# A two-layer decoder kernel on one core: the second chunk of the down weights in two parts, and the routing weights computed earlier

## The chip, the core and the metric

The kernel runs on one core of one Trainium2 chip. The core has a matrix engine (PE, with weight loads listed apart as PEld), three engines for elementwise work (DVE, ACT and POOL), and queues for DMA, most of which are issued by SP. Each engine works through its own instructions in the order in which they were written; semaphores make an instruction wait for another engine. The metric is the device time of one execution in microseconds (us).

## The reference

Two layers work on 512 tokens of width 1024, all in float32. Each layer has a mixing part (four mixers, one output projection), a mixture of experts, and a gated embedding. The change lies in the mixture of experts:

```python
def hier_moe(x, wg, bg, we, be, w_gate, w_up, w_down):
    gl = jnp.einsum("bsd,dg->bsg", x, wg, ...) + bg          # 4 groups
    pg = jax.nn.softmax(gl, axis=-1)
    c = jnp.argmax(gl, axis=-1)
    el = ...                                                 # 4 experts of the group
    pe = jax.nn.softmax(el_c, axis=-1)
    tv, ti = lax.top_k(pe, TOP_K_IN_GROUP)                   # 2 of them
    tv = tv / jnp.sum(tv, axis=-1, keepdims=True)
    wts = gc * tv
    ...
    for e in range(N_EXPERTS):                               # 16
        hdn = jax.nn.silu(x @ w_gate[e]) * (x @ w_up[e])     # 1024 -> 256
        y = y + combine[..., e:e + 1] * (hdn @ w_down[e])    # 256 -> 1024
```

## The kernel before

Tokens lie in four tiles of 128. After the routing (`route`, L1064) the kernel goes through the 16 experts in a fixed order (`experts`, L1282). For each it gathers up to 128 rows of its tokens from DRAM (an indirect DMA issued by POOL), transposes them on PE, multiplies by the gate and up weights, applies silu, multiplies by the down weights and scatters the result (another indirect DMA of POOL). Tokens beyond 128 of an expert go through `overflow`.

A matrix product is made in one of two ways. In the one (`mm3`, L254) both factors are split into a high part of type F32R and a low part, the difference, also F32R; three multiplies, high by high, high by low and low by high, are added up in PSUM. The high part of a weight tile is a cast on ACT (`whi_of`, L224), the low part a subtraction on DVE (`wlo_of`, L235). In the other way the product is one multiply of F32 tiles, which needs no splitting.

The weights come in units of 128x2048 F32 (1 MB), loaded by SP into rings of buffers (`wr` in the rows). An expert has three units: two of gate and up, each used as two halves of 128x1024, and one of down, whose first half (rows 0 to 127 of the 256) is split, and whose second half is used as F32. `_Weights.get` (L137) hands out the halves in order and makes high parts three halves ahead, low parts right after, into rings `wh` and `wl` of four tiles each.

The loop over e is skewed: iteration e does gate and up of expert e in four quarters q (six multiplies each), and the down product of expert e-1 at its end. After quarter 1, `down_in` (L1215) transposes the silu result `hs` of expert e-1; its first 128 columns are split into `hh` (a cast on ACT, a subtraction on DVE), its second 128 copied to `hT` (DVE). After quarter 3 come silu of expert e (`eth` on ACT, `ehs` twice on DVE) and the transposes and split of the next gathered rows (`xTh` on ACT, `xTl` on DVE, L222). Then `down` (L1229): for the first chunk of 128 rows, three F32R multiplies for each of the two halves of 512 columns (L255 to L257); for the second chunk, one F32 multiply for each half (L1241). ACT evicts the result (`ys`), POOL scatters it. Iteration 16 has the last expert's down product alone.

`weights` (L1131) computes the two weights of a token's experts, nine small operations on DVE and two exponentials on ACT; it is called at the start of iteration 2, and its result is first used in `combine` (L1330), after all experts.

The order of the work is the order of the program's text; no scheduler moves it.

Of the kernel before, what the change touches and what calls it, by code (L numbers as in the profile page):

```python
# [11 lines left out]
F32 = mybir.dt.float32  # L12
F32R = mybir.dt.float32r
# [154 lines left out]
class _Kernel:  # L168
# [895 lines left out]
    def route(self):  # L1064
        nc, V, G, T, SC, sm, l = self.nc, self.V, self.G, self.T, self.SC, self.sm, self.l
        iota, L, small = self.iota, self.L, self.small
        ep = self.ep = self.pool("ep", side=self.side[1])
        self.xg = [self.gpool.tile([128, D], F32, name=f"xg{j}", tag=f"gv{1 - j}") for j in range(2)]
        for j in range(2):
            G.memset(self.xg[j], 0.0)  # L1070
        self.yd = self.dram.tile([2 * S, D], F32, name=f"yd{l}")

        Cz = small([128, NT + 1, 16], "Cz", BF)
        G.memset(Cz[:, 0], 0.0)

        L5 = L.rearrange("p i (g e) -> p i g e", e=4)
        O1, O2 = small([128, NT, 5, 4], "O1"), small([128, NT, 4, 4], "O2")
        el = small([128, NT, 4, 4], "el")
        m1 = self.first_max(O1, L5, 5, "o1")
        V.scalar_tensor_tensor(el, O1[:, :, 1:], -BIG, L5[:, :, 1:], op0=ALU.mult, op1=ALU.add)  # L1080
        m2 = self.first_max(O2, el, 4, "o2")
        og = O1[:, :, 0, :, None].to_broadcast([128, NT, 4, 4])
        V.tensor_add(el, O1[:, :, 1:], O2)
        V.tensor_mul(Cz[:, 1:].rearrange("p i (g e) -> p i g e", e=4), el, og)
        OH = small([128, 2, NT, 16], "OH")
        for k, src in enumerate((O1[:, :, 1:], O2)):
            V.tensor_mul(OH[:, k].rearrange("p i (g e) -> p i g e", e=4), src, og)

        pc = self.mm([128, NT + 1, 16])
        T.matmul(pc, self.onesb, Cz, start=True, stop=False)  # L1090
        for j in range(2, NT + 1):
            T.matmul(pc[:, j:], self.onesb, Cz[:, 1:NT + 2 - j], start=False, stop=False)
        T.matmul(pc[:, 0:NT], self.trib, Cz[:, 1:], start=False, stop=True)

        OH8 = OH.rearrange("p k i e -> p (k i) e")
        RO = small([128, 8, 2, 16], "RO", F16)
        V.tensor_mul(RO, OH8[:, :, None, :].to_broadcast([128, 8, 2, 16]),
                     self.vtab[:, :, :, None].to_broadcast([128, 8, 2, 16]))
        pk = small([128, 8, 16], "pk")
        V.tensor_mul(pk.rearrange("p (k i) e -> p k i e", k=2), OH,  # L1100
                     pc[:, None, 0:NT].to_broadcast([128, 2, NT, 16]))
        pos = small([128, 8], "pos")
        V.tensor_reduce(pos, pk, axis=AX, op=ALU.add)
        SO = ep.tile([128, 8, 128], F16, name="SO", tag="ys", bufs=2)
        pidx = self.mm([128, 32])
        for a in (0, 4):
            V.tensor_tensor(SO[:, a:a + 4], iota[:, None, :].to_broadcast([128, 4, 128]),
                            pos[:, a:a + 4, None].to_broadcast([128, 4, 128]), op=ALU.is_equal)
            for j in range(a, a + 4):
                T.matmul(pidx, SO[:, j], RO[:, j].rearrange("p a e -> p (a e)"), start=(j == 0), stop=(j == 7))  # L1110
        ix = self.ix = self.mp.tile([128, 32], I32, name="ix")
        V.tensor_scalar(ix, pidx, NOIDX, None, op0=ALU.add)
        for e in range(2):
            self.gather(self.xg[e], ix[:, e:e + 1])

        nov = self.nov = small([128, NE], "nov")
        V.tensor_scalar(nov, pc[:, NT], 128.5, None, op0=ALU.is_ge)
        for lim in (256.5, 384.5):
            V.scalar_tensor_tensor(nov, pc[:, NT], lim, nov, op0=ALU.is_ge, op1=ALU.add)
        novs = small([128, 1], "novs")  # L1120
        V.tensor_reduce(novs, nov, axis=AX, op=ALU.add)
        self.novi = small([128, 1], "novi", I32)
        V.tensor_copy(self.novi, novs)
        self.cnt = small([128, 1], "cnt")
        V.memset(self.cnt, 0.0)
        self.w.make_lo()
        self.warm(WARM)
        self.OH8, self.pos = OH8, pos
        self.wt_in = L[:, :, 0:4], m1, m2, O1[:, :, 0]

    def weights(self):  # L1131

# [79 lines left out]
        self.V.tensor_mul(hs, hs, gu[:, 256:512])  # L1212
        return hs

    def down_in(self, hs, split=True):  # L1215

        pt = self.tr([128, 2, 128])
        for c in range(2):
            self.T.transpose(pt[:, c], hs[:, c * 128:(c + 1) * 128], self.ident)
        hT = self.ep.tile([128, 2, 128], F32, name="hT", bufs=2)  # L1220
        if not split:
            self.V.tensor_copy(hT, pt)
            return hT, None
        hh = self.ep.tile([128, 2, 128], F32R, name="hh", bufs=2)
        self.split(pt[:, 0], hh[:, 0], hh[:, 1])
        self.V.tensor_copy(hT[:, 1], pt[:, 1])
        return hT, hh

    def down(self, hT, w_, first=None):  # L1229

        hT, hh = hT
        ys = self.ep.tile([128, D], F32, name="ys", bufs=2)
        o = [self.mm([128, 512]) for _ in range(2)]
        for c in range(2):
            wc = first if first and not c else w_(c)
            for nh in range(2):
                ns = slice(nh * 512, (nh + 1) * 512)
                if first and not c:
                    self.mm3(o[nh], hh[:, 0], hh[:, 1], wc[0][:, ns], wc[1][:, ns], True, False)
                else:  # L1240
                    self.T.matmul(o[nh], hT[:, c], wc[:, ns], start=(c == 0), stop=(c == 1))  # L1241
        for nh in range(2):
            self.SC.activation(ys[:, nh * 512:(nh + 1) * 512], o[nh], AF.Copy, scale=0.5)  # L1243
        return ys

    def overflow(self):
# [4 lines left out]
        with tc.If(n_ov > 0) as _:  # L1251
            with tc.For_i(0, n_ov, 1) as _:
                ixo, eovi = self.block()
                ex = nc.values_load(eovi[:1, 0:1], engines=[mybir.EngineType.SP], min_val=0, max_val=NE - 1,
                                    skip_runtime_bounds_check_because="an expert's index")
                og = ep.tile([128, D], F32, name="og", tag="ys", bufs=2)
                G.memset(og, 0.0)
                self.gather(og, ixo[:, 0:1])
                oT = ep.tile([128, 8, 128], F32, name="oT", tag="xTh", bufs=1)
                for b in range(2):  # L1260
                    pt = self.tr([128, 4, 128])
                    for c in range(4):
                        T.transpose(pt[:, c], og[:, (4 * b + c) * 128:(4 * b + c + 1) * 128], self.ident)
                    V.tensor_copy(oT[:, 4 * b:4 * b + 4], pt)
                gu = self.mm([128, 512])

                def part(src, c):
                    w_ = ep.tile([128, 1024], F32, name="ow", tag="xTl", bufs=1)
                    src = src.rearrange("a p n -> p (a n)")
                    nc.sync.dma_start(w_, src[:, c * 1024:(c + 1) * 1024])  # L1270
                    return w_

                for q in range(4):
                    w_ = part(A["wgu"][l, bass.ds(ex, 1), q // 2], q % 2)
                    for c in range(2):
                        T.matmul(gu, oT[:, 2 * q + c], w_[:, c * 512:(c + 1) * 512], start=(q + c == 0), stop=(q + c == 4))
                hs = self.silu(gu)
                ys = self.down(self.down_in(hs, False), lambda c: part(A["wdn"][l, bass.ds(ex, 1)], c))
                self.scatter(ys, ixo[:, 1:2])


    def experts(self):  # L1282
# [12 lines left out]
        w.load(w.items[w.cur][0] + 1 + w.ahead, self.G)  # L1295
        prep(0)
        for e in range(NE + 1):
            if e == 2:
                self.weights()
            if e == NE - 1:  # L1300
                self.gbias = self.gvec(3 * l + 2, 1)
                self.pT = self.gpool.tile([128, 2, S], F32, name="pT", tag="gv0")
# [1 line left out]
            if e == NE - 1 and l + 1 < self.depth:  # L1304
                self.load_params(l + 1)
            if e < NE:
                hiT, loT = xT.pop(e)
                gu = self.mm([128, 512])
                for q in range(4):
# [3 lines left out]
                        self.mm3(gu, hiT[:, k], loT[:, k], hi[:, c], lo[:, c], k == 0, k == 7)  # L1313
                    if q == 1 and e > 0:
                        hT = self.down_in(hs)
                hs = self.silu(gu)
            else:
                hT = self.down_in(hs)
            if e + 1 < NE:
                prep(e + 1)  # L1320
            if e > 0:
                first, wd = w.get(), w.get()
                ys = self.down(hT, lambda c: wd[:, c * 1024:(c + 1) * 1024], first)
                si = self.scatter(ys, self.ix[:, 16 + e - 1:16 + e])
                for s_ in scat:
                    tc.declare_no_dep(si.ins, s_.ins, reason="rows of other tokens or ranks")
# [254 lines left out]
```

## Time and profile before

| | us |
|---|---|
| median of 3 runs (lowest, highest) | 904.88 (903.62, 905.17) |
| the profiled execution, its own time | 907.17 |
| its span from first to last instruction | 905.3 |
| PE busy in the span | 850.8 (94%) |
| DVE busy | 706.5 (78%) |
| ACT busy | 514.3 (57%) |
| POOL busy | 158.2 (17%) |

The experts of the two layers lie at about 229 to 388 and 671 to 830 us of the span. "Busy" is the time in which an engine executes; register work, semaphores and DMA issues don't count. A row of the timeline has the start, the time it took, engine, line, operation, the tile it writes and those it reads, the shape, the count, and in brackets the idle time before it and what ended that. Neighbouring rows overlap by a little, since an engine starts an instruction before the last one has drained; for PE the starts tell more than the durations. A row "x2" stands for two instructions one behind the other. An F32 multiply of 512 columns has two records, an F32R multiply one.

### The profile page before, as it was taken

What the parts mean: (1) busy time and instruction counts of PE and PEld (TensorE: products, weight loads), DVE (VectorE), ACT (ScalarE), POOL (GpSimd) and SP (SyncE); (2) the same over time, 40 slices, a digit from 0 to 9 for tenths busy, and PEclk for the clock granted to TensorE, in tenths of its full rate; (3) what the DMA queues carried; (4) which work ended last, traced back from release to release, by engine and by line L of the source; (5) the groups of instructions that cost most, each with busy time, mean ns of one, the idle gap of its engine ahead of it and who ended that gap; (6) DMA issues with size and microseconds to landing.
All of it is one profiled execution on the core that took longest, in us unless ns stands there. A gap on an engine that the chain in (4) does not pass through costs nothing. (4 is left out here: it accounts for less than half of the span.)

```text
span 905.3 us, 12251 instructions
## 1 busy us (share of the span) xinstructions
PE 850.8 (94%) x4393; PEld 683.9 (76%) x4393; DVE 706.5 (78%) x1182; ACT 514.3 (57%) x929; POOL 158.2 (17%) x214
## 2 busy tenths in 40 slices
PE   6999999997899999999979999999969999999994
PEld 5888877785677777777879887778847777777783
DVE  4499989966788888766676999898478888885674
ACT  4322348753677877755433232696447778777453
POOL 2050002122221221011010500112132122111201
PEclk8999999997999999999999999999979999999998
DMA  9322330157799979663322212210968998882702
GB/s 341 120 102 76 122 117 1 47 219 293 267 337 358 375 275 333 268 245 161 117 93 93 94 62 106 100 48 31 392 225 310 364 374 320 316 325 92 274 24 93
DMA packets 35776, 179.02 MB, mean 198 GB/s; under 512 B 8064, under 2 KB 8320, under 8 KB 18944
## 3 DMA queue, kind: packets, MB, share of 16 engines
q1 hardware_dynamic: 23472, 148.49, 43.7%
q0 software_dynamic: 9792, 20.99, 6.3%
q10 hardware_dynamic: 2448, 8.73, 2.6%
q8 instruction: 35, 0.57, 0.2%
q14 instruction: 29, 0.24, 0.1%
HBM read 171.89 MB, written 23.07 MB: 215 GB/s over the span
## 5 line engine op out<-in xcount | busy, mean ns | idle before, releaser
L239 DVE TENSOR_TENSOR wl<-wr,wh 128x1024 fp32r<-128x1024 f32 x212 | 253.2, 1221 | 43.0 <-ACT wh L228 41.8
L228 ACT CAST wh<-wr 128x1024 fp32r<-128x1024 f32 x212 | 216.4, 1053 | 89.9 <-PE mm L256 52.2
L255 PE MATMUL mm<-wh,xTh 128*128 128x512 f32 x256 | 114.4, 447 | 0.7 <-ACT xTh L221 0.7
L257 PE MATMUL mm<-wh,xTl 128*128 128x512 f32 x256 | 101.5, 396 | 1.2 <-DVE xTl L222 1.2
L256 PE MATMUL mm<-wl,xTh 128*128 128x512 f32 x256 | 100.9, 394 | 0.0
L483 DVE SCALAR_TENSOR_TENSOR acc<-glu,cwh,acc 128x512 f32<-128x512 f32 x120 | 91.7, 830 | 0.1
L257 PE MATMUL mm<-nhi,wl 128*128 128x512 f32 (+1 forms) x224 | 77.3, 345 | 2.6 <-DVE wl L239 2.6
L255 PE MATMUL mm<-nhi,wh 128*128 128x512 f32 (+1 forms) x224 | 77.1, 344 | 0.0
L256 PE MATMUL mm<-nlo,wh 128*128 128x512 f32 (+1 forms) x224 | 77.0, 344 | 0.0
L1198 POOL DMA_INDIRECT xg<-xnd,ix x32 | 35.3, 1105 | 150.2 <-PE tr L251 137.9
L255 PEld LDWEIGHTS mm<-wh,xTh 128*128 128x128 f32 x256 | 48.5, 190 | 16.7 <-issue 6.7
L1241 PE MATMUL mm<-wr,hT 128*128 128x512 f32 x128 | 60.2, 592 | 0.0
L256 PEld LDWEIGHTS mm<-wl,xTh 128*128 128x128 f32 x256 | 48.5, 190 | 15.4 <-DVE wl L239 6.2
L257 PEld LDWEIGHTS mm<-wh,xTl 128*128 128x128 f32 x256 | 48.3, 189 | 12.8 <-DVE xTl L222 2.7
L255 PE MATMUL mm<-wh,mhi 128*128 128x512 f32 x128 | 54.9, 429 | 0.0
L1203 POOL DMA_INDIRECT yd<-ys,ix x32 | 32.3, 1010 | 122.9 <-ACT ys L1243 107.3
L255 PE MATMUL mm<-wh,n3h 128*128 128x512 f32 x128 | 51.1, 399 | 0.0
L257 PE MATMUL mm<-wh,mlo 128*128 128x512 f32 x128 | 50.9, 397 | 0.0
L256 PE MATMUL mm<-wl,mhi 128*128 128x512 f32 x128 | 50.5, 394 | 0.0
L257 PE MATMUL mm<-wh,n3l 128*128 128x512 f32 x128 | 50.4, 394 | 0.0
L256 PE MATMUL mm<-wl,n3h 128*128 128x512 f32 x128 | 49.9, 390 | 0.0
L257 PEld LDWEIGHTS mm<-nhi,wl 128*128 128x128 f32 x224 | 42.4, 189 | 8.2 <-DVE wl L239 3.2
(235 smaller groups left out, 1851.2 us busy)
## 6 DMA issues: line engine op xcount, KB each, us to landing
wr<-wgu SPq DMA_DIRECT2D x62, 1024.0 KB, 9.1
wr<-wdn SPq DMA_DIRECT2D x30, 1024.0 KB, 13.4
wr<-win SPq DMA_DIRECT2D x13, 1024.0 KB, 9.4
wr<-wout SPq DMA_DIRECT2D x8, 1024.0 KB, 4.9
wr<-wpg SPq DMA_DIRECT2D x8, 1024.0 KB, 15.8
yt<-yd SPq DMA_DIRECT2D x12, 512.0 KB, 8.0
wr<-wqk SPq DMA_DIRECT2D x4, 1024.0 KB, 4.7
xnd<-xn ACTq DMA_DIRECT2D x8, 512.0 KB, 3.7
```

Source lines behind the costliest of these rows:

```text
L228: self.SC.copy(hi, src)
L239: self.V.tensor_sub(lo, src, h32)
L255: self.T.matmul(o, lh, rh, start=first, stop=False)
L256: self.T.matmul(o, lh, rl, start=False, stop=False)
L257: self.T.matmul(o, ll, rh, start=False, stop=last)
L483: V.scalar_tensor_tensor(acc[:, m], glu[:, m, k:k + S], self.cwh[:, m, k:k + 1], acc[:, m], op0=ALU.mult, op1=ALU.add)
L1198: return self.G.indirect_dma_start(out=dst, out_offset=None, in_=self.xnd[:, :], in_offset=bass.IndirectOffsetOnAxis(ap=col, axis=0), boun ...
L1203: return self.G.indirect_dma_start(out=self.yd[:, :], out_offset=bass.IndirectOffsetOnAxis(ap=col, axis=0), in_=src, in_offset=None, bound ...
L1241: self.T.matmul(o[nh], hT[:, c], wc[:, ns], start=(c == 0), stop=(c == 1))
```

## The change

For iterations 1 to 15 the second chunk of the down weights is also split in two parts and multiplied with `mm3`. A new function `down2` makes the parts, in two halves of 512 columns: both high parts are casts on ACT; the low part of the first half is a subtraction on POOL (`self.G`), that of the second half a subtraction on DVE. They have tiles of their own with one buffer each (`w2h0`, `w2l0`, `w2h1`, `w2l1`, in the rows of the order `w2h` and `w2l` with a number). The call for the first half stands after quarter 1 (behind `down_in`), that for the second after quarter 2. `down_in` splits both chunks of the transposed activations in these iterations, in one cast and one subtraction of 128x256, and makes no copy. Iteration 16, the last expert, and the overflow keep the old way. `weights()` is called at the end of `route` instead of at iteration 2.

```diff
         self.wt_in = L[:, :, 0:4], m1, m2, O1[:, :, 0]
+        self.weights()
...
+        hh = self.ep.tile([128, 2, 2, 128], F32R, name="hh", bufs=2)
+        if split == 2:
+            self.split(pt, hh[:, 0], hh[:, 1])
+            return None, hh
+        self.split(pt[:, 0], hh[:, 0, 0], hh[:, 1, 0])
+        hT = self.ep.tile([128, 2, 128], F32, name="hT", tag="eth", bufs=2)
         self.V.tensor_copy(hT[:, 1], pt[:, 1])
         return hT, hh

-    def down(self, hT, w_, first=None):
+    def down2(self, u, nh):
+
+        hi, lo = (self.ep.tile([128, 512], F32R, name=f"w2{a}{nh}", bufs=1) for a in "hl")
+        src = self.w.raw[u][:, 1024 + nh * 512:1536 + nh * 512]
+        self.SC.copy(hi, src)
+        (self.V if nh else self.G).tensor_sub(lo, src, hi.bitcast(F32))
+        return hi, lo
+
+    def down(self, hT, w_, first=None, second=None):
...
-                if first and not c:
-                    self.mm3(o[nh], hh[:, 0], hh[:, 1], wc[0][:, ns], wc[1][:, ns], True, False)
+                if second if c else first:
+                    hi, lo = second[nh] if c else (t[:, ns] for t in first)
+                    self.mm3(o[nh], hh[:, 0, c], hh[:, 1, c], hi, lo, c == 0, c == 1)
                 else:
                     self.T.matmul(o[nh], hT[:, c], wc[:, ns], start=(c == 0), stop=(c == 1))
...
-            if e == 2:
-                self.weights()
...
                     if q == 1 and e > 0:
                         hT = self.down_in(hs)
+                    if q in (1, 2) and e > 0:
+                        second.append(self.down2(w.items[w.cur + 3 - q][0], q - 1))
                 hs = self.silu(gu)
             else:
-                hT = self.down_in(hs)
+                second = None
+                hT = self.down_in(hs, 1)
```

On ACT, one iteration of the experts before, from silu on (`eth`: silu's tanh; `xTh`: high part of the next gathered rows; `wh`: high parts of weights; `ys`: evicted down product; `hh`: transposed activations):

```order
L1209 ACTIVATE eth<-mm 128x256
L221 CAST xTh<-tr 128x512 x2
L228 CAST wh<-wr 128x1024 x2
L1243 ACTIVATE ys<-mm 128x512 x2
L228 CAST wh<-wr 128x1024 x2
L221 CAST hh<-tr 128x128
L228 CAST wh<-wr 128x1024
```

The same of the changed kernel:

```order
L1210 ACTIVATE eth<-mm 128x256
L221 CAST xTh<-tr 128x512 x2
L228 CAST wh<-wr 128x1024 x2
L1257 ACTIVATE ys<-mm 128x512 x2
L228 CAST wh<-wr 128x1024 x2
L221 CAST hh<-tr 128x256
L1238 CAST w2h_2629<-wr 128x512
L1238 CAST w2h_2641<-wr 128x512
L228 CAST wh<-wr 128x1024
```

The two new casts stand between the cast of the activations, now twice as wide, and the last cast of weights before silu.

On DVE, one iteration before, from silu on (`ehs`: silu; `xTl`: low part of the gathered rows; `wl`: low parts of weights):

```order
L1211 SCALAR_TENSOR_TENSOR ehs<-eth,mm 128x256
L1212 TENSOR_TENSOR ehs<-ehs,mm 128x256
L222 TENSOR_TENSOR xTl<-tr,xTh 128x512 x2
L239 TENSOR_TENSOR wl<-wr,wh 128x1024 x4
L222 TENSOR_TENSOR hh<-tr,hh 128x128
L1226 COPY hT<-tr 128x128
L239 TENSOR_TENSOR wl<-wr,wh 128x1024
```

The same of the changed kernel:

```order
L1212 SCALAR_TENSOR_TENSOR ehs<-eth,mm 128x256
L1213 TENSOR_TENSOR ehs<-ehs,mm 128x256
L222 TENSOR_TENSOR xTl<-tr,xTh 128x512 x2
L239 TENSOR_TENSOR wl<-wr,wh 128x1024 x4
L222 TENSOR_TENSOR hh<-tr,hh 128x256
L1239 TENSOR_TENSOR w2l_2860<-wr,w2h_2859 128x512
L239 TENSOR_TENSOR wl<-wr,wh 128x1024
```

The copy is gone, the subtraction of the activations is twice as wide, and the low part of the second half stands behind it. In POOL's queue the other low part stands ahead of the gather and the scatter of each iteration, where before the two followed each other alone.

On DVE at the end of the routing, the difference between the two kernels, from the last low parts of weights made there to the first gathered rows:

```order
 L239 TENSOR_TENSOR wl<-wr,wh 128x1024 x3
-L222 TENSOR_TENSOR xTl<-tr,xTh 128x512 x2
-L239 TENSOR_TENSOR wl<-wr,wh 128x1024 x4
-L1211 SCALAR_TENSOR_TENSOR ehs<-eth,mm 128x256
-L1212 TENSOR_TENSOR ehs<-ehs,mm 128x256
+L1137 TENSOR_TENSOR gd<-L,o1x 128x16
+L1139 TENSOR_TENSOR dg<-o2x,o1x 128x16
+L1140 TENSOR_TENSOR dg<-dg,O_2299 128x16
+L1142 TENSOR_REDUCE d_2389<-dg 128x4
+L1146 TENSOR_REDUCE sg<-gd 128x4
+L1147 SCALAR_TENSOR_TENSOR sg<-d_2389,sg 128x4
```

The operations of `weights` (six of the nine are shown) now stand ahead of the first expert's `xTl`, and the two exponentials on ACT ahead of its `xTh`.

## Rows read from the trace of the kernel before

**Rows 1.** Table of stages: busy us (count) of each engine, granted clock, DMA share, GB/s.
```profile
262.00:372.00 110.00, 110.00 (x504) 83.83 (x502) 93.55 (x126) 84.41 (x124) 21.18 (x21) 1.00 0.91 343
690.00:810.00 120.00, 120.00 (x544) 91.29 (x543) 103.11 (x145) 93.56 (x138) 24.42 (x24) 1.00 0.91 340
```
**Rows 2.** Waits of PE from 232 to 392: us in total, times, longest.
```profile
PE mm L255 <- ACT hh L221: 0.6, 1, 0.6
PE mm L257 <- DVE xTl L222: 0.6, 1, 0.6
```
**Rows 3.** Timeline of DVE, one iteration: start us, us, line, tiles, idle before.
```profile
279.69 2.36 DVE L239 TENSOR_TENSOR wl<-wr,wh 128x1024 fp32r<-128x1024 f32 x2 [0.70 <-ACT wh L228]
281.96 0.28 DVE L222 TENSOR_TENSOR hh<-tr,hh 128x128 fp32r<-128x128 f32 x1
...
282.36 1.22 DVE L239 TENSOR_TENSOR wl<-wr,wh 128x1024 fp32r<-128x1024 f32 x1
284.27 0.42 DVE L1211 SCALAR_TENSOR_TENSOR ehs<-eth,mm 128x256 f32<-128x256 f32 x1 [0.69 <-ACT eth L1209]
...
285.06 1.28 DVE L222 TENSOR_TENSOR xTl<-tr,xTh 128x512 fp32r<-128x512 f32 x2
286.34 2.36 DVE L239 TENSOR_TENSOR wl<-wr,wh 128x1024 fp32r<-128x1024 f32 x2
289.41 2.36 DVE L239 TENSOR_TENSOR wl<-wr,wh 128x1024 fp32r<-128x1024 f32 x2 [0.70 <-ACT wh L228]
```
**Rows 4.** Timeline of PE around L1241: in mid-stage, and at the last experts.
```profile
276.20 1.88 PE L1241 MATMUL mm<-wr,hT 128*128 128x512 f32 x4
...
278.15 0.40 PE L256 MATMUL mm<-wl,xTh 128*128 128x512 f32 x1
278.38 0.40 PE L257 MATMUL mm<-wh,xTl 128*128 128x512 f32 x1
...
382.28 1.88 PE L1241 MATMUL mm<-wr,hT 128*128 128x512 f32 x4
383.99 0.38 PE L1219 MATMUL tr<-con,ehs 128*128 128x128 f32 x2
```
**Rows 5.** Timeline of ACT in the same iteration.
```profile
281.10 0.27 ACT L221 CAST hh<-tr 128x128 fp32r<-128x128 f32 x1 [0.50 <-PE tr L1219]
281.26 1.05 ACT L228 CAST wh<-wr 128x1024 fp32r<-128x1024 f32 x1
283.85 0.38 ACT L1209 ACTIVATE eth<-mm 128x256 f32<-128x256 f32 x1 [1.54 <-PE mm L257]
```
**Rows 6.** Groups by line and form, count | busy us, mean ns | idle before.
```profile
L221 ACT CAST mhi<-yd 128x512 fp32r<-128x512 f32 x4 | 2.5, 620 | 10.6 <-DVE yd L581 10.6
...
L222 DVE TENSOR_TENSOR mlo<-yd,mhi 128x512 fp32r<-128x512 f32 x4 | 2.8, 692 | 2.7 <-ACT mhi L221 2.7
```
**Rows 7.** Timeline of POOL in the same iteration: the gather of later rows.
```profile
284.96 1.01 POOL L1198 DMA_INDIRECT xg<-xnd,ix  x1 [4.96 <-PE tr L251]
```
**Rows 8.** Timelines of DVE and POOL in the first layer's convolution.
```profile
58.13 0.74 DVE L483 SCALAR_TENSOR_TENSOR acc<-glu,cwh,acc 128x512 f32<-128x512 f32 x1
...
58.21 1.58 POOL L513 TENSOR_TENSOR sB<-sA 64x526 f32<-64x526 f32 x1
...
58.79 1.55 DVE L483 SCALAR_TENSOR_TENSOR acc<-glu,cwh,acc 128x512 f32<-128x512 f32 x1
```
**Rows 9.** Timeline of DVE: ends of both routings, first and ninth operation of `weights`.
```profile
229.95 0.69 DVE L222 TENSOR_TENSOR xTl<-tr,xTh 128x512 fp32r<-128x512 f32 x1 [2.69 <-ACT xTh L221]
...
249.72 0.17 DVE L1136 TENSOR_TENSOR gd<-L,o1x 128x16 f32<-128x16 f32 x1
...
251.12 0.16 DVE L1151 TENSOR_TENSOR wts<-wts,d 128x4 f32<-128x4 f32 x1
...
672.28 1.29 DVE L222 TENSOR_TENSOR xTl<-tr,xTh 128x512 fp32r<-128x512 f32 x2 [2.23 <-ACT xTh L221]
```
**Rows 10.** Timeline of DVE in iteration 15 of the first layer.
```profile
377.82 2.36 DVE L239 TENSOR_TENSOR wl<-wr,wh 128x1024 fp32r<-128x1024 f32 x2 [1.57 <-ACT wh L228]
```

More of the change, by code (lines that the diff above doesn't have):

```diff
@@ L1213, in silu, with down_in @@
         return hs
-    def down_in(self, hs, split=True):
+    def down_in(self, hs, split=2):
         pt = self.tr([128, 2, 128])
@@ L1219, in down_in @@
             self.T.transpose(pt[:, c], hs[:, c * 128:(c + 1) * 128], self.ident)
-        hT = self.ep.tile([128, 2, 128], F32, name="hT", bufs=2)
         if not split:
+            hT = self.ep.tile([128, 2, 128], F32, name="hT", tag="hh", bufs=2)
             self.V.tensor_copy(hT, pt)
             return hT, None
-        hh = self.ep.tile([128, 2, 128], F32R, name="hh", bufs=2)
-        self.split(pt[:, 0], hh[:, 0], hh[:, 1])
+        hh = self.ep.tile([128, 2, 2, 128], F32R, name="hh", bufs=2)
[4 more added lines that the diff above has]
+        hT = self.ep.tile([128, 2, 128], F32, name="hT", tag="eth", bufs=2)
         self.V.tensor_copy(hT[:, 1], pt[:, 1])
         return hT, hh
-    def down(self, hT, w_, first=None):
+    def down2(self, u, nh):
[5 more added lines that the diff above has]
+    def down(self, hT, w_, first=None, second=None):
         hT, hh = hT
@@ L1234, in down @@
         for c in range(2):
-            wc = first if first and not c else w_(c)
+            wc = None if (second if c else first) else w_(c)
             for nh in range(2):
                 ns = slice(nh * 512, (nh + 1) * 512)
-                if first and not c:
-                    self.mm3(o[nh], hh[:, 0], hh[:, 1], wc[0][:, ns], wc[1][:, ns], True, False)
+                if second if c else first:
+                    hi, lo = second[nh] if c else (t[:, ns] for t in first)
+                    self.mm3(o[nh], hh[:, 0, c], hh[:, 1, c], hi, lo, c == 0, c == 1)
                 else:
@@ L1277, in overflow @@
                 hs = self.silu(gu)
-                ys = self.down(self.down_in(hs, False), lambda c: part(A["wdn"][l, bass.ds(ex, 1)], c))
+                ys = self.down(self.down_in(hs, 0), lambda c: part(A["wdn"][l, bass.ds(ex, 1)], c))
                 self.scatter(ys, ixo[:, 1:2])
@@ L1306, in experts @@
             if e < NE:
+                second = []
                 hiT, loT = xT.pop(e)
@@ L1322, in experts @@
                 first, wd = w.get(), w.get()
-                ys = self.down(hT, lambda c: wd[:, c * 1024:(c + 1) * 1024], first)
+                ys = self.down(hT, lambda c: wd[:, c * 1024:(c + 1) * 1024], first, second)
                 si = self.scatter(ys, self.ix[:, 16 + e - 1:16 + e])
```

## The prediction

> **What bounds the kernel now.** [...] One expert takes 9.72 us (the same DVE row starts at 279.69 and at 289.41) [rows 3].
>
> **The gain on PE.** An F32 multiply (L1241) runs as two records: four records for the two halves of the second chunk. At the last expert nothing but them stands between 382.28 and the next transpose at 383.99, so they take 1.71 us; in the middle of the stage, 276.20 to 278.15 holds the four and one L255, 1.95 - 0.23 = 1.72 [rows 4]. A multiply in F32R with 512 columns follows its neighbour after 278.38 - 278.15 = 0.23 us [rows 4]. Six of them in their place take 1.38. That is 0.33 us less for each expert, and the change does it for 15 experts in each of two layers: 30 x 0.33 = **9.9 us**, and the period would be 9.39.
>
> **What ACT takes on.** In one period it idles 0.50 (until the transposed activations) and 1.54 (until the last gate/up multiply) [rows 5], so it works 9.72 - 2.04 = 7.68. Added are two casts of 128x512 from SBUF, 0.62 each [rows 6], of which 0.09 overlaps the next instruction: 1.06; and the cast of the transposed activations doubles to 128x256, 0.38 for that form against 0.27 [rows 5]: 0.11. Sum 8.85 of 9.39. With the 1.05 of the next 128x1024 [rows 5] the four casts in a row after 281.10 end at about 283.5, before the 283.85 at which ACT has to take the gate/up result. Covered; without the cover each extra 0.1 us there would be 3 us in all.
>
> **What DVE takes on.** Its period has two idle pieces, 0.69 and 0.70 [rows 3]; with the ends that overlap where no idle follows, its work packed tight is 8.16. The 128x128 difference and the 128x128 copy (281.96 to 282.36, 0.40) become one difference of 128x256, 0.42 for that form [rows 3], 0.34 net: -0.06. The low half of 128x512, both inputs in SBUF, is 0.69 [rows 6], 0.61 net. Sum 8.16 - 0.06 + 0.61 = 8.71.
>
> **What POOL takes on, and the lock.** The other low half goes to POOL, a two-input operation of 128x512. POOL has the room: it idles 4.96 us before the gather at 284.96 [rows 7], the cast it waits for ends at about 282.0, and its result is wanted only at about 286. The next gather and the scatter stay behind it in POOL's queue, and neither would be late by it at 2.0 us. But another stretch shows what such an operation does to DVE [rows 8]: the tap at 58.13 takes 0.74; POOL's two-input add starts at 58.21; the next, equal tap takes 1.55, so DVE was held 0.81 us. This repeats for five of the six adds of that stretch. All of DVE's weight differences (L239) have both inputs in SBUF as the taps do, while its differences from PSUM have one. The trace has no such POOL operation beside L239, so I bound the hold: from below 0 (POOL falls into a stretch of PSUM work), from above 1.58, POOL's own record, of which 0.66 was its wait for the earlier tap. I take 0.81, the row nearest in form (526 columns against 512). Of it 0.34 falls beside the 128x256 difference from PSUM, which stands just there: 0.47 remain, and DVE comes to 9.18 of 9.39. PE stays the bound, with 0.2 us to spare. The consumer that feels it first is the low half of the next expert's second quarter: in the kernel before it is done at 287.56 [rows 3] and wanted at 278.15 + 6 x 0.23 + 9.72 = 289.25; by my walk through the queues it lands about 0.8 us ahead, not 1.7.
>
> [...]
>
> **The other edits.** The routing weights, nine small DVE operations and two of ACT, take 1.56 us (249.72 to the end of the ninth at 251.28) [rows 9]. PE did not wait for them there, so taking them away gives nothing. At the end of the routing DVE idles 2.69 us before 229.95 [rows 9] (2.23 in the other layer), and ACT waits longer still for the gathered rows; both work them off there. Cost nothing; if the gather came sooner, up to 1.56 a layer. The last expert keeps the old path. One iteration ahead of it ACT also issues three loads, and DVE waited 1.57 instead of 0.70 [rows 10]; with less slack that can reach PE. I put 0.2 us a layer on it, 0.4 in all (bounds 0 and 0.87 a layer). The loads: a raw down tile is free some 3 us sooner than when PE read it. The stage moves 343 GB/s at a share of 0.91 [rows 1], 377 at full share; the shorter period asks for 343 x 9.72 / 9.39 = 355. It fits.
>
> **The sum.** -9.9 + 0.4 = -9.5 us. The profiled execution took 907.17 us (span 905.3, the rest around it), so 897.7 by its own time; it was 2.3 us above the median of the runs, 904.88, and the prediction is against that: **895.4**.
>
> **The rivals.**
> DVE becomes the bound in part. If the full 0.81 falls on two-input work, DVE needs 8.71 + 0.81 = 9.52 against 9.39: 0.13 x 30 = 3.9 of the gain go, 899.3. For it: DVE packed tight has no idle piece in which to take the hold. Against: the cast that releases POOL ends just before the PSUM difference.
> [...]
> The change does not do what it says: PE's records shrink, but ACT's chain fills the period, which stays at 9.72, 904.9. ACT would need 0.87 more than the rows give, from waits between its casts.
>
> **How the numbers follow.** PE stays the bound: 0.74, 895.4, and 893.0 to 897.5 with the scatter of runs and the bounds of the last-expert term. DVE in part: 0.10, 897.5 to 902. Lock dearer than the gain: 0.10, 904 to 912. No gain: 0.06. The range 893.0 to 900.5 leaves out about 0.2. A measurement of this kernel can tell about 0.2%, 1.8 us, from no change: faster 0.84, same 0.06, slower 0.10.
>
> **What would show it.** In the profile after: periods of 9.39 (DVE's rows 9.39 apart), PE busy throughout the experts, six F32R records in place of the four; DVE's 128x512 low half longer than 0.69 by some of the hold, and idle pieces of DVE nearly gone; ACT idle about 0.5 a period. Waits of PE for a low half (wl) in mid-stage would say that DVE is the bound; waits for the halves made by POOL that POOL is late. I am wrong if POOL's record is well over 1.4 with DVE held as long.

## The result, and the profile after

The changed kernel took 895.38 us (median; 894.96 to 898.0) where the kernel before took 905.02 (903.62 to 907.32) on the same chip: a ratio of 0.9885, 95% interval 0.9866 to 0.9904. Beside the kernel before on another chip it gave 0.9887 (0.9865 to 0.9909). The profiled execution of it had a span of 896.2 us, against 905.3; its own time, 898.0, is the longest of the four.

The head of the page after, with the busy time of each engine:

```profile
span 896.2 us, 12495 instructions
...
PE 842.7 (94%) x4453; PEld 696.2 (78%) x4453; DVE 738.3 (82%) x1182; ACT 545.9 (61%) x989; POOL 228.5 (25%) x244
```

PE is busy 8.1 us less than before (850.8) with 60 more records; DVE is busy 31.8 us more, ACT 31.6 and POOL 70.3. The table of stages after, in the middle of each layer's experts (columns as in [rows 1]):

```profile
262.00:362.00 100.00, 100.00 (x495) 83.09 (x494) 99.62 (x119) 92.02 (x141) 46.24 (x31) 1.00 0.93 354
680.00:800.00 120.00, 120.00 (x593) 99.67 (x592) 119.15 (x142) 110.49 (x168) 54.92 (x38) 1.00 0.93 351
```

PE is still full at a granted clock of 1.00, as in [rows 1]. But DVE, which had 93.55 of 110 us there, is now full too: 99.62 of 100. ACT has 92.02, and the loads move 354 GB/s. The waits of PE over the first layer's experts (total, times, longest):

```profile
PE mm L257 <- DVE xTl L222: 0.6, 1, 0.6
PE mm L255 <- ACT hh L221: 0.4, 1, 0.4
PE mm L255 <- ACT xTh L221: 0.2, 1, 0.2
PE tr L1220 <- DVE ehs L1213: 0.2, 1, 0.2
```

Against [rows 2] there is nothing new but 0.2 us at the last expert. No low part of weights stands among them: a full DVE has not made PE wait.

PE in mid-stage, from the last multiply of the first chunk (275.62) to the first of the next expert (277.22); the four multiplies between 275.85 and 277.00 are left out:

```profile
275.62 0.40 PE L257 MATMUL mm<-wh,hh 128*128 128x512 f32 x1
275.85 0.39 PE L255 MATMUL mm<-w2h,hh 128*128 128x512 f32 x1
...
277.00 0.39 PE L257 MATMUL mm<-w2h,hh 128*128 128x512 f32 x1
277.22 0.39 PE L255 MATMUL mm<-wh,xTh 128*128 128x512 f32 x1
...
282.92 1.03 PE L251 MATMUL tr<-con,xg 128*128 128x128 f32 x8
```

The six multiplies of the second chunk take 277.22 - 275.85 = 1.37 us where the four records took 1.72 [rows 4]. The transposes at 282.92 stood at 273.58 in the expert before: a period of 9.34, where it was 9.72 by DVE's rows [rows 3] and 9.73 by PE's.

DVE, one iteration after (answers to [rows 3]):

```profile
272.13 0.42 DVE L222 TENSOR_TENSOR hh<-tr,hh 128x256 fp32r<-128x256 f32 x1
272.47 1.45 DVE L1239 TENSOR_TENSOR w2l<-wr,w2h 128x512 fp32r<-128x512 f32 x1
273.85 1.21 DVE L239 TENSOR_TENSOR wl<-wr,wh 128x1024 fp32r<-128x1024 f32 x1
...
276.96 4.62 DVE L239 TENSOR_TENSOR wl<-wr,wh 128x1024 fp32r<-128x1024 f32 x4
281.50 0.42 DVE L222 TENSOR_TENSOR hh<-tr,hh 128x256 fp32r<-128x256 f32 x1
281.83 1.46 DVE L1239 TENSOR_TENSOR w2l<-wr,w2h 128x512 fp32r<-128x512 f32 x1
```

No row has an idle piece in brackets any more. The low part of the second half of columns (L1239, the low half from here on) takes 1.45 instead of the 0.69 of its form [rows 6]; the weight differences of 128x1024 around it (L239, the wide differences) keep their 1.21. DVE's own period is 281.50 - 272.13 = 9.37, 0.03 more than PE's.

POOL in the same stretch (answers to [rows 7]):

```profile
269.11 1.72 POOL L1204 DMA_INDIRECT yd<-ys,ix  x1 [2.53 <-ACT ys L1257]
272.00 1.37 POOL L1239 TENSOR_TENSOR w2l<-wr,w2h 128x512 fp32r<-128x512 f32 x1 [1.18 <-ACT w2h L1238]
```

POOL waits 1.18 us for the cast; its low half begins 0.13 us before DVE's wide difference ends (the end of a row that has no idle time behind it is taken as the start of the next, here 272.13), and DVE's low half falls into it. And ACT (answers to [rows 5]):

```profile
271.02 0.37 ACT L221 CAST hh<-tr 128x256 fp32r<-128x256 f32 x1 [0.31 <-PE tr L1220]
271.29 1.15 ACT L1238 CAST w2h<-wr 128x512 fp32r<-128x512 f32 x2
272.34 1.06 ACT L228 CAST wh<-wr 128x1024 fp32r<-128x1024 f32 x1
273.78 0.38 ACT L1210 ACTIVATE eth<-mm 128x256 f32<-128x256 f32 x1 [0.39 <-PE mm L257]
```

ACT idles 0.31 + 0.39 a period, so it works 8.64 of 9.34.

### The profile page after: what moved, and what is told of

The parts are those of the page before. It is cut to its first block, busy times and chain, and to the rows that moved or that the text cites. A ratio compares the mean times of both kernels' runs of the same rounds, so it can differ in the third digit from the quotient of the medians.

```text
span 896.2 us, 12495 instructions
## 1 busy us (share of the span) xinstructions
PE 842.7 (94%) x4453; PEld 696.2 (78%) x4453; DVE 738.3 (82%) x1182; ACT 545.9 (61%) x989; POOL 228.5 (25%) x244
## 5 line engine op out<-in xcount | busy, mean ns | idle before, releaser
L239 DVE TENSOR_TENSOR wl<-wr,wh 128x1024 fp32r<-128x1024 f32 x212 | 250.5, 1219 | 24.1 <-ACT wh L228 23.5
L255 PE MATMUL mm<-wh,xTh 128*128 128x512 f32 x256 | 103.7, 405 | 0.7 <-ACT xTh L221 0.7
L1204 POOL DMA_INDIRECT yd<-ys,ix x32 | 55.3, 1729 | 91.2 <-ACT ys L1257 69.2
L1199 POOL DMA_INDIRECT xg<-xnd,ix x32 | 38.2, 1194 | 64.3 <-PE tr L251 51.5
L1239 POOL TENSOR_TENSOR w2l<-wr,w2h 128x512 fp32r<-128x512 f32 x30 | 44.3, 1477 | 38.2 <-ACT w2h L1238 38.2
```

Of the source, the lines that this page charges most:

```text
L239: self.V.tensor_sub(lo, src, h32)
L255: self.T.matmul(o, lh, rh, start=first, stop=False)
L1199: return self.G.indirect_dma_start(out=dst, out_offset=None, in_=self.xnd[:, :], in_offset=bass.IndirectOffsetOnAxis(ap=col, axis=0), boun ...
L1204: return self.G.indirect_dma_start(out=self.yd[:, :], out_offset=bass.IndirectOffsetOnAxis(ap=col, axis=0), in_=src, in_offset=None, bound ...
L1239: (self.V if nh else self.G).tensor_sub(lo, src, hi.bitcast(F32))
```

## The experiments

All were run beside the kernel before on one chip per group: the first four together, the next three together, and the last three together.

**The weights of the routing moved, alone.** The kernel before with `weights()` at the end of the routing:

```
         self.wt_in = L[:, :, 0:4], m1, m2, O1[:, :, 0]
+        self.weights()
...
-            if e == 2:
-                self.weights()
```

> The kernel before with the routing weights moved to the end of the routing, and nothing else. Theory (the gain is PE's cheaper multiplies; the nine small DVE operations kept PE from nothing where they stood): 904.9, within 0.5 us of the kernel before, experts still 9.73 us apart. Rival (freeing DVE early in the experts is part of the gain): 1 to 3 us faster.

Measured: 906.8 us, ratio 1.0002 (0.9985 to 1.0019); periods 9.73. In the kernel before the move is worth nothing, as its rows had said: DVE waits at the new place [rows 9], and PE did not wait at the old one [rows 2].

**The split alone.** The changed kernel with `weights()` back at iteration 2:

```
-        self.weights()
...
+            if e == 2:
+                self.weights()
```

> The changed kernel with the routing weights back at iteration 2. In the changed kernel DVE has no idle piece left (period 9.37 against PE's 9.34), and its lead over PE at the second quarter's low half falls from 0.71 to 0.35 us over the experts. Theory: 1.56 us of DVE work put back there can't be made up, so PE waits for wl: 1.56 - 0.35 = about 1.2 us a layer, 2.4 in all, 897.8; the waits stand in the trace from iteration 2 on. Rival (the move is worth nothing in either kernel, as my prediction had it): 895.4, no waits of PE.

Measured: 897.84 us, ratio 0.9911 (0.9894 to 0.9928), some 2.4 us behind the changed kernel by the ratios; the two intervals overlap, so the trace has to tell it. In each layer two periods are 10.33 and 9.73 instead of 9.34, 1.38 us in all, and the twelve behind them are 9.36 on average, another 0.27; PE waits for low parts of weights, which it does in neither whole kernel. The first row is from the waits of PE, the others are the first and the ninth of the small operations on DVE:

```profile
PE mm L256 <- DVE wl L239: 0.7, 2, 0.4
```
```profile
249.39 0.17 DVE L1136 TENSOR_TENSOR gd<-L,o1x 128x16 f32<-128x16 f32 x1
...
250.75 0.16 DVE L1151 TENSOR_TENSOR wts<-wts,d 128x4 f32<-128x4 f32 x1
```

So the two edits belong together: with the split DVE has no idle piece left in which the nine operations could be worked off. Behind them the period is close to the 9.37 that DVE needs in the changed kernel: this is the prediction's rival of DVE as the bound in part.

**Both low parts on DVE.** The changed kernel, nothing on POOL:

```
-        (self.V if nh else self.G).tensor_sub(lo, src, hi.bitcast(F32))
+        self.V.tensor_sub(lo, src, hi.bitcast(F32))
```

> The changed kernel with both low halves of the second chunk on DVE, none on POOL. Theory (POOL's subtraction holds DVE by 0.77 us, more than the 0.61 that DVE would need to do the half itself): DVE's period 9.37 - 0.77 + 0.61 = 9.21, under PE's 9.34, so its lead no longer falls and idle pieces of 0.1 come back; the time stays at 895.4 within 0.7, since PE is the bound. Rival (POOL takes 0.61 us off DVE): DVE would need 9.37 + 0.61 = 9.98 a period, 0.64 x 28 = 18 us slower, 913.

Measured: 896.23 us, ratio 0.989 (0.9873 to 0.9907), equal to the changed kernel; periods 9.34. The table of stages, and DVE's two low parts:

```profile
262.00:362.00 100.00, 100.00 (x495) 83.11 (x494) 99.07 (x131) 92.02 (x140) 25.60 (x21) 1.00 0.93 355
```
```profile
271.62 1.28 DVE L1239 TENSOR_TENSOR w2l<-wr,w2h 128x512 fp32r<-128x512 f32 x2
```

Two such parts of its own take DVE 1.28 us; one of its own beside one of POOL's takes it 1.45. DVE is busy 99.07 of 100 us here and 99.62 in the changed kernel. Handing half of the work to POOL saves DVE nothing: it stands still for 0.77 us, and the half would have taken it 0.61. What that does can be followed in the lead of one low part of weights, the one that PE takes in an expert's second quarter (from its end on DVE to the start of the first multiply that reads it). Here the lead stays at 0.86 us from the second expert of the stage to the last; in the changed kernel it falls from 0.72 to 0.36 over fourteen experts.

**Both low parts on POOL.**

```
-        (self.V if nh else self.G).tensor_sub(lo, src, hi.bitcast(F32))
+        self.G.tensor_sub(lo, src, hi.bitcast(F32))
```

> The changed kernel with both low halves on POOL. Theory (each POOL subtraction holds DVE's two-input work by about 1.0 us, of which 0.3 lie beside work from PSUM once): DVE needs 9.37 - 1.38 + 1.7 = 9.7 a period, over PE's 9.34: after the lead of 0.7 us is used up PE waits for wl, 0.35 x 28 - 1.4 = 8.4 us slower than the changed kernel, 904. Rival (work handed to POOL frees DVE): 895.4 or a little less, DVE idle 0.6 a period.

Measured: 897.55 us, ratio 0.9913 (0.9896 to 0.9929), about 2.5 us behind the changed kernel by the ratios instead of the 8.4 expected. The periods alternate between 9.48 and 9.34, so PE loses 0.14 in every second iteration, 2 us in all, which is most of that difference. Two iterations, POOL and DVE:

```profile
270.08 4.10 POOL L1239 TENSOR_TENSOR w2l<-wr,w2h 128x512 fp32r<-128x512 f32 x2 [1.83 <-ACT w2h L1238]
...
279.44 2.56 POOL L1239 TENSOR_TENSOR w2l<-wr,w2h 128x512 fp32r<-128x512 f32 x2 [1.29 <-ACT w2h L1238]
```
```profile
271.50 1.52 DVE L239 TENSOR_TENSOR wl<-wr,wh 128x1024 fp32r<-128x1024 f32 x1 [0.39 <-ACT wh L228]
...
280.86 2.23 DVE L239 TENSOR_TENSOR wl<-wr,wh 128x1024 fp32r<-128x1024 f32 x1 [0.92 <-ACT wh L228]
```

In one iteration DVE's wide difference comes between POOL's two, loses 0.3, and POOL waits (4.10 for the two); in the next it comes behind the first and loses 1.0, while POOL needs 2.56. The expectation charged both holds to DVE's two-input work in every iteration, some 1.7 us; it is 0.65 on average. The rest falls beside DVE's differences from PSUM (the one of 128x256 inside POOL's row at 270.08 takes 0.42, no more than elsewhere) and into its waits for ACT (0.39, 0.92), where it costs DVE nothing. So here DVE is not full, 92.99 of the same 100 us, and PE still waits: the low part that PE takes in the second quarter, made behind the one that was held, has a lead of only 0.05 us in every second expert.

**Half of the split.** Only the second half of the columns is split, the first half stays one F32 multiply (so the copy to `hT` on DVE is there again), POOL does nothing:

```
-            return None, hh
+            hT = self.ep.tile([128, 2, 128], F32, name="hT", tag="eth", bufs=2)
+            self.V.tensor_copy(hT[:, 1], pt[:, 1])
+            return hT, hh
...
-                if second if c else first:
+                if (second and second[nh]) if c else first:
...
-                    if q in (1, 2) and e > 0:
+                    if q == 1 and e > 0:
+                        second.append(None)
+                    if q == 2 and e > 0:
                         second.append(self.down2(w.items[w.cur + 3 - q][0], q - 1))
```

> The changed kernel, but only the second half of columns of the second chunk is split (casts on ACT, low part on DVE, nothing on POOL); the first half stays one F32 multiply. Theory that the gain is PE's instruction time: one F32 multiply has two records of 0.43 us, three F32R multiplies take 0.68 to 0.70, so the period falls by about 0.17 to 0.2, from 9.73 to 9.53 or 9.56, about half the gain of the whole change: 900.5 to 901. Rival, that the extra 0.06 of gain per expert over the prediction (0.39 instead of 0.33) comes from a change of kind between F32 and F32R that is gone altogether only when no F32 multiply is left: then the half gains 0.33/2 = 0.165 and no more, a period of 9.56 and 901. The two differ by 0.03 in the period, which the trace tells apart. DVE has room (idle of some 0.6 a period), so no wait of PE in mid-stage by either.

Measured: 900.2 us, ratio 0.9916 (0.9894 to 0.9939), the kernel before at 907.33 on that chip. By the periods it is decided: 9.53 in both layers, half of the way from 9.73 to 9.34. PE around the F32 multiply:

```profile
275.06 1.02 PE L1257 MATMUL mm<-wr,hT 128*128 128x512 f32 x2
...
276.62 0.39 PE L255 MATMUL mm<-wh,xTh 128*128 128x512 f32 x1
```

From 275.06 to 276.62 the F32 multiply and three F32R ones take 1.56; less three of 0.23 the F32 multiply takes 0.87, and the three that replace it 0.68. The gain is PE's instruction time, nearly in proportion to what is split; the rival, a price of the change of kind that goes only with the last F32 multiply, is out.

**The hold of POOL by itself.** The kernel before, with one subtraction more on POOL in each of iterations 1 to 15; its result is not used:

```
+                    if q == 1 and e > 0:
+                        n = 512 if e % 2 else 256
+                        src = w.raw[w.items[w.cur + 2][0]][:, 1024:1024 + n]
+                        lo = ep.tile([128, n], F32R, name=f"w2l{e % 2}", bufs=1)
+                        self.G.tensor_sub(lo, src, src)
```

> The kernel before, with one more two-input subtraction on POOL in each of iterations 1 to 15, whose result is not used: of 128x512 in odd iterations and 128x256 in even ones, both inputs in SBUF. This measures the hold by itself. Theory: POOL holds DVE for the whole of its own execution, about 1.0 us at 512 columns and about 0.5 at 256, so that the DVE instruction that meets it is longer by that much. Rival one (the prediction's value from the convolution): 0.8 and 0.4. Rival two: the hold is one fixed price for each meeting whatever the size, so equal at 512 and 256. DVE idles 1.4 us a period here, so the time stays that of the kernel before, within 0.2%, by every theory.

Measured: 906.15 us, ratio 0.9992 (0.9971 to 1.0013), no change, as expected with DVE's idle pieces there. An even and an odd iteration, DVE and POOL:

```profile
269.40 1.66 DVE L239 TENSOR_TENSOR wl<-wr,wh 128x1024 fp32r<-128x1024 f32 x1 [0.27 <-ACT wh L228]
...
270.98 1.63 DVE L239 TENSOR_TENSOR wl<-wr,wh 128x1024 fp32r<-128x1024 f32 x1
...
279.12 2.49 DVE L239 TENSOR_TENSOR wl<-wr,wh 128x1024 fp32r<-128x1024 f32 x1 [0.71 <-ACT wh L228]
```
```profile
270.04 1.48 POOL L1320 TENSOR_TENSOR w2l<-wr 128x256 fp32r<-128x256 f32 x1
...
279.46 1.06 POOL L1320 TENSOR_TENSOR w2l<-wr 128x512 fp32r<-128x512 f32 x1
```

A wide difference takes 1.22 alone. With 512 columns on POOL one is held 1.27; with 256, two of them are held 0.44 and 0.41, 0.85 together. None of the three expectations: 256 columns more cost 0.42, which would make 0.84 for 512, and another 0.43 does not depend on the size. Where that 0.43 comes from stays open: in this kernel POOL's subtraction stands right behind the scatter, and DVE is held from 279.12, 0.34 before the subtraction's record begins. So this run shows that POOL's subtraction holds DVE with no other change in the kernel, but not its price away from a scatter.

**The last expert too, and more fillers.** Two candidates for a better kernel: both low parts on DVE and the last expert's second chunk split as well, and the same with 14 instead of 11 filler multiplies (multiplies whose result is not used) at the end of the routing (`WARM`). The second was run twice, and the changed kernel once more beside them. The edit of the second; the first leaves out its first two lines:

```
-WARM0, WARM, PRE = 17, 11, 7
+WARM0, WARM, PRE = 17, 14, 7
...
-        (self.V if nh else self.G).tensor_sub(lo, src, hi.bitcast(F32))
+        self.V.tensor_sub(lo, src, hi.bitcast(F32))
...
-                second = None
-                hT = self.down_in(hs, 1)
+                hT = self.down_in(hs)
+                second = [self.down2(w.items[w.cur + 1][0], nh) for nh in range(2)]
```

> Both low parts on DVE as in the earlier run of that kind, the last expert's second chunk split too, and 14 instead of 11 filler multiplies at the end of the routing. Theory: the last expert gains 0.35 in each layer; the fillers end about 1.3 us later, at the arrival of the first gathered rows, so the granted clock reaches 1.00 some 1.3 us sooner in the layer whose first gate/up multiplies now run at 0.50 (nine of them 0.43 apart instead of 0.23, 1.8 us), which gives 0 to 1.8 there and nothing in the other layer. Together 0.7 to 2.5 us under the kernel with both low parts on DVE (896.2): 893.7 to 895.5. Rival: the clock follows something else and the fillers only delay the first transposes, up to 0.5 us a layer: 895.9 to 896.5.

> The changed kernel itself once more, beside the two candidates on the same chip. Theory: ratio 0.9885 as in the first comparison, periods of 9.34. It also tells whether the slow first multiplies of the first layer's experts (granted clock 0.50 there in the first profile) belong to this kernel or only to that execution: if the kernel, the clock between 230 and 235 us is again near 0.56; if the execution, it can be anything from 0.56 to 1.00.

> Both low parts on DVE and the last expert split too, with the 11 filler multiplies of the changed kernel. Theory: the last expert gains 0.35 in each layer over the kernel with both low parts on DVE, 0.7 in all, which the trace shows and the times hardly; against the changed kernel the saving is the same 0.7 or up to 1 (no lead is lost on DVE): a ratio of 0.9875 to 0.988.

> The same with 14 fillers, a second time and on the same chip as the kernel with 11. If the fillers raise the clock where the first gathered rows are multiplied, this is 0.5 to 1.8 us below the kernel with 11 and its clock from 230 to 235 us is 1.00; if the clock there differs from execution to execution whatever the fillers, the two agree within 0.5 us.

Measured: with 14 fillers first 894.61 us, ratio 0.9853 (0.9829 to 0.9877), beside the half split; then on the chip of the other two 896.09, 0.9899 (0.9874 to 0.9923), against 896.09, 0.9895 (0.9875 to 0.9915) with 11 fillers, and 895.87, 0.9887 for the changed kernel. Nothing here is shown to beat the changed kernel: the ratio of 0.9853 did not come back. The last expert's gain itself is there; PE between the second chunk's first multiply and the next stage, with 11 fillers:

```profile
380.54 0.39 PE L255 MATMUL mm<-w2h,hh 128*128 128x512 f32 x1
...
381.91 1.46 PE L1364 MATMUL mm<-wr,pT 128*128 128x256 f32 x6
```

1.37 where the F32 multiplies took 1.72, so 0.35 a layer in the block; from the last silu's tanh to the next stage 0.25 of it is left (6.50 us, against 6.75 in the kernel with both low parts on DVE), too little for the times to show. As to the fillers, the granted clock of 230 to 235 us was 0.74 in the kernel before and 0.66 in the second execution of the changed one. The same stretch (the clock stands ahead of the last two columns) in the first execution of the changed kernel, with 11 fillers, and with 14:

```profile
230.00:235.00 5.00, 5.00 (x14) 3.90 (x14) 3.50 (x4) 2.58 (x3) 1.05 (x1) 0.56 1.01 401
```
```profile
230.00:235.00 5.00, 4.76 (x21) 3.47 (x20) 3.74 (x4) 4.03 (x5) 1.05 (x1) 1.00 0.95 385
```
```profile
230.00:235.00 5.00, 4.98 (x21) 3.82 (x22) 4.25 (x5) 3.74 (x5) 1.05 (x1) 1.00 0.99 406
```

It was 1.00 with 11 fillers as with 14, and it differs between two executions of the same kernel. In the kernel with both low parts on POOL, whose program up to there is that of the changed kernel, two casts of ACT that waited for PE's multiplies there start 234.25 - 232.89 = 1.36 apart, which is six multiplies of 0.23. So no effect of the fillers on the clock is shown, and the clock there is part of the scatter of all these kernels.

## Why the prediction came out right, and which of its terms did not

The forecast was 895.4, the median is 895.38. The direction and the mechanism hold: PE stayed the bound (it was that before by [rows 1] and [rows 2]), and its shorter instructions are the gain. That the two numbers agree to 0.02 us is luck. The interval of the ratio alone is 1.7 us to either side, the experts gained 1.9 us more than forecast (11.4 against 9.5), some of that was lost again where the prediction had no term, and the time that DVE needs was wrong in two parts.

**PE's instructions (0.33 an expert predicted, 0.39 measured).** The period fell by 9.73 - 9.34 = 0.39: the fourteen full periods of a layer together by 5.41, from 136.17 to 130.76, where 0.33 each would have given 4.6. The block itself gained 1.72 - 1.37 = 0.35: six multiplies follow each other after 0.228 each, and the step that took 0.23 from [rows 4] rounded that up, 6 x 0.23 = 1.38. The remaining 0.03 to 0.04 lies in the multiplies of the next expert behind the block: their starts were 0.231 apart on average before and are 0.227 apart after. Starts of up to 0.236 apart stand behind the transposes in both kernels too, for some eight multiplies; before, they stood behind the F32 records as well. Why is not shown; the half split rules out that the gain takes a kernel without any F32 multiply.

**DVE (9.18 predicted, 9.37 measured).** Two errors. The work packed tight was put at 8.71; with both low parts on DVE it idles some 0.14 of 9.34 (in one place the starts of two wide differences are that much further apart than elsewhere), so it works 9.20 with one low half of 0.60 more, and 8.60 is the true value of that term. Of the 0.11 too much, 0.08 stands in [rows 3]: the wide difference at 286.34 starts only as `xTl` ends (285.06 + 1.28), where rows with no wait between them overlap by 0.08. That was a wait for ACT, and it was counted as work. Against that the hold was put at 0.47 net, from the 0.81 of [rows 8], and is 0.77: 1.46 against 0.69 [rows 6]. The hold itself is longer than 0.81. POOL's record starts at 272.00, DVE's wide difference ends at about 272.13, and DVE's low half, without a hold 0.6 long, ends at 273.85, so it got its data at about 273.24. By an estimate from these rows the hold lasts 273.24 - 272.13 = 1.1 us, 0.34 of it beside the PSUM difference, as the step said: that one takes 0.42 beside POOL, as its form does in [rows 3]. What makes it longer than the row of the convolution is not shown. It is not that row's 64 partitions: an add of 128x527 at 60.35 held the next tap as long, 1.55 us in all. The output type is another here, and the two inputs are two tiles. But the prediction counted five of six adds of that stretch, and the sixth (64x520) held its tap 1.05:

```profile
67.80 1.79 DVE L483 SCALAR_TENSOR_TENSOR acc<-glu,cwh,acc 128x512 f32<-128x512 f32 x1
```

With that row DVE would have come to 9.42, over PE's 9.39: the step of this term that failed is the choice of the row nearest in columns where a longer one stood beside it.

So "PE stays the bound, with 0.2 us to spare" was wrong in its second half. DVE needs 0.03 more than PE, and the lead of the low part that PE takes in the second quarter falls from 0.72 us to 0.36 over the fourteen experts. It was predicted at about 0.8 us, and that lead is what hid the deficit: the stage ends before it is used up. The rival of DVE as the bound in part was nearer than its chance of 0.10 says. An estimate from these rows: at 0.03 us an expert the 0.36 left would last for twelve more, so with twice the experts in a layer it would have come, as it did in the kernel with the split alone, where the nine operations used the lead up.

**The rivals with a loss.** "Lock dearer than the gain" (0.10) needed a DVE over 9.72, so by the numbers of the prediction a hold over 9.72 - 8.71 + 0.34 = 1.35. What the runs show is a hold of 1.1 by the estimate above, beside a POOL record of 1.37. ACT filling the period needed 0.87 us more of work than the rows gave; ACT works 8.64, less than the 8.85 predicted: the two evictions `ys` start 0.70 apart before and 0.49 after, and that wait had been counted as work.

**The weights.** "Cost nothing" held: at the new place DVE still waits 1.79 us for the gathered rows in the changed kernel's first layer. "Taking them away gives nothing" held for the kernel before, where the run alone shows it; it does not hold beside the split, where leaving them in costs some 2.4 us. The prediction had priced the two edits apart.

**The last expert (a loss of 0.4 in all predicted).** In the first layer the starts of silu's tanh and of the first multiply of the last down product are 380.16 - 376.52 = 3.64 apart, before 385.00 - 381.12 = 3.88, so 0.24 less. The split takes 0.35 out between them, and 0.11 was given back. In the second layer they are 3.53 apart instead of 3.88, and nothing was given back. The term was 0.1 for both layers. In the first layer the cause is the one named, DVE late with `ehs`:

```profile
379.40 0.41 PE L1220 MATMUL tr<-con,ehs 128*128 128x128 f32 x2 [0.21 <-DVE ehs L1213]
...
380.16 0.50 PE L255 MATMUL mm<-wh,hh 128*128 128x512 f32 x1 [0.35 <-ACT hh L221]
```

**The sum.** Twice 5.41 for the full periods, and 0.23 and 0.35 from the last silu's tanh to the next stage, make -11.4 for the experts of both layers; the two ratios of the changed kernel give -10.3 of 905. The profiled spans differ by 9.1. Of what is missing in them 1.4 us lies at the start of the first layer's experts, where the first multiplies stood 0.43 apart instead of 0.23 for longer; from 232 to 234 us the granted clock was 0.50, before 0.84:

```profile
233.44 0.63 PE L257 MATMUL mm<-wh,xTl 128*128 128x512 f32 x1
233.87 0.63 PE L255 MATMUL mm<-wh,xTh 128*128 128x512 f32 x1
```

The execution of the same kernel on the other chip had a span of 894.1, 2.1 less, and lost 0.3 there instead of 1.4, so this belongs to the execution. Another part belongs to the change. Behind the second layer's experts PE now waits for the sum `h`, which DVE makes only when the load of the scattered rows (`yt`) has landed (it waits 6.19 and 0.44 us for two pieces of it):

```profile
826.93 2.23 SPq L1382 DMA_DIRECT2D yt<-yd  x5
832.30 0.63 PE L251 MATMUL tr<-con,h 128*128 128x128 f32 x4 [0.68 <-DVE h L1391]
```

The load is issued 7.08 us behind the first multiply of that stage (819.85), where it was 6.39 before (835.96 and 829.57), and PE did not wait there. The second execution of the changed kernel shows the same, with a wait of 0.5. So 0.5 to 0.7 us of what the experts gained is lost behind them, a term that the prediction did not have. What stays between that and 10.3 is inside the intervals.

## What to carry to other kernels

Count an engine's free time as one budget for the whole change: two edits of which one frees time on an engine and the other fills it can have one price together and another apart, as here, where the move of the weights gave nothing alone and some 2.4 us beside the split. Where a low part is handed to POOL while DVE works on two SBUF inputs, ask what DVE saves after the hold, and what DVE does meanwhile: where its two-input work met the hold it saved nothing (0.77 us held for 0.61 of work taken off), and beside its work from PSUM (0.42 as without it) or its waits the hold cost it nothing. When two engines come out as near to each other as here, 9.37 and 9.34 us a period, the lead at the start of the stage and the number of periods decide, so work out both. And follow the gain past the end of the stage: the next one may wait for something that did not get faster.

## What was not expected of the hardware

An indirect DMA issued by POOL took longer when it began inside one of DVE's wide differences. Its record is some 1.0 us in the kernel before (1010 ns on average for the scatter), and 1729 ns in the changed one. Three cases, POOL's row and the row of DVE that was running (1.13 us from its start to that of the next): a scatter in the changed kernel is the 269.11 of the POOL rows above, beside

```profile
268.72 1.22 DVE L239 TENSOR_TENSOR wl<-wr,wh 128x1024 fp32r<-128x1024 f32 x1
```

a scatter with both low parts on DVE, so without any elementwise work on POOL,

```profile
277.66 1.51 POOL L1204 DMA_INDIRECT yd<-ys,ix  x1 [2.55 <-ACT ys L1257]
```
```profile
277.07 1.22 DVE L239 TENSOR_TENSOR wl<-wr,wh 128x1024 fp32r<-128x1024 f32 x1
```

and a gather in the kernel with the split alone:

```profile
274.55 1.53 POOL L1198 DMA_INDIRECT xg<-xnd,ix  x1 [1.05 <-PE tr L251]
```
```profile
273.97 1.21 DVE L239 TENSOR_TENSOR wl<-wr,wh 128x1024 fp32r<-128x1024 f32 x1
```

What was left of DVE's instruction when POOL's began is 0.74, 0.54 and 0.55 us, and the records are 0.72, 0.51 and 0.53 longer than 1.0. The indirect DMAs thus wait for the running instruction, as POOL's own low half does (1.37 with 0.13 left; 1.83 with 0.60 left in the kernel with the split alone). The same holds for all 52 indirect DMAs of the changed kernel's experts that begin inside a wide difference: what is left runs from 0.01 to 1.15 us, and the records are longer than 1.0 by that less up to 0.14. Those that begin inside `xTl`, whose one input is in PSUM, are not longer: with 0.6 left they take 1.02 in the kernel with both low parts on POOL. DVE's next instruction is not held: a wide difference behind the scatter keeps its 1.22. In mid-stage this cost nothing, since POOL has time (busy 46.24 of 100 us in the changed kernel). At the end of the routing, in both kernels, the gather that PE waits for begins inside a wide difference too, and is 2.33 us long in the changed one, more than the 1.07 left there explains:

```profile
223.21 2.33 POOL L1199 DMA_INDIRECT xg<-xnd,ix  x1 [6.27 <-DVE cnt L1125]
228.07 1.97 PE L251 MATMUL tr<-con,xg 128*128 128x128 f32 x8 [1.29 <-DMA xg<-xnd,ix]
```

How much of PE's 1.29 us goes back to that no run here shows; one that makes these differences behind the gather would.
